# The norms of a two-layer decoder trunk: VectorE's work in a written order, one inverse deviation for both token chunks

## The chip, the cores and the metric

One core of a Trainium2 chip runs the whole kernel. The metric is device time in microseconds of one execution; for the kernel before it is the median of 3 runs. A profile is one further execution, recorded by the hardware profiler; its span runs from the first instruction to the last, and its own time also holds what lies around the span.

TensorE (PE, with PEld for its weight loads) does the matmuls and transposes, VectorE (DVE) elementwise work and reductions, ScalarE (ACT) copies, casts and functions, GpSimd (POOL) the rest, and SyncE (SP) issues nearly all transfers in one queue.

## The reference, cut to what matters

256 tokens of width 1024 go through two layers. Layer 0 is dilated attention, layer 1 attention over a compressed, a selected and a sliding-window branch of one shared set of keys and values. Each layer is followed by 16 experts, of which a token uses 2.

```
def layer_norm(x, g, b):
    mu = mean(x, axis=-1)
    var = mean(square(x - mu), axis=-1)
    return (x - mu) * rsqrt(var + 1e-5) * g + b

for layer in range(2):
    if layer == 0:
        mix = dilated_attention(h, ...)
    else:
        shared_kv = nsa_shared_kv(h, w_kv, ...)      # projections of h: the first work of layer 1
        mix = nsa_attention(h, w_q, ..., *shared_kv)
    h = layer_norm(ALPHA * h + mix, ln_mix_g[layer], ln_mix_b[layer])
    h = layer_norm(ALPHA * h + hier_moe(h, ...), ln_ffn_g[layer], ln_ffn_b[layer])
```

## The kernel before

The tokens are two chunks (c = 0, 1) of 128 partitions. A matmul in the precision that is wanted takes three: each operand is split into a high part (a cast to fp32r, on ScalarE) and a low part (a subtraction, on VectorE), and the products high-high, high-low and low-high are summed. `split` does it for a weight of 128x2048 in four pieces (wh on ScalarE, L251, wl on VectorE, L252), and its results lie in a pool of 4 tiles ("hl"). `projT` and `projN` multiply such a weight with the token matrix: 32 matmuls with wh first, then 16 with wl.

Weights come through one list (`stream`). `take()` gives the next tile of it and loads ahead: as many tiles as `st["ahead"]` says, all from SP's queue in the list's order. Most of them and other wide tiles share a pool of 13 buffers ("u": x, the wkv, w1 and wq weights, lngb, F, KH, KL, VV, qS and others). A load waits in SP's queue until its buffer is free.

A scheduler orders each engine's instructions ahead of time. Inside `tc.manual_schedule(engines=...)` the named engines keep the order of the program text instead; the kernel uses that for TensorE (`PES`) in several places. PSUM tiles for products come from `B("A", ...)`, which here goes round four banks (tags A, A, Y, R).

Between the layers the following happens, in the order of the program. The last experts' outputs are added into x by `scatter(3)` (PSUM tiles sps, L735), which gives the row sums too; 38 matmuls that compute nothing (`awake(38)`) follow on TensorE. For each chunk: the negated mean (`neg_mean`, L477), the squares with their sums (`squares`, ScalarE, L487), z = (x + nm) * g (L956), the inverse deviation by `rstd` (a start value by integer arithmetic and three Newton rounds, on 128x1 columns; on GpSimd for chunk 0 and on VectorE for chunk 1, L495 to L501), z = z * y + b (L960), and 8 transposes of z into two PSUM tiles (hps, L557). Each of these tiles is read three times by `evac`: hTH (ScalarE, L965), hTL (VectorE, L966) and hT (ScalarE, L967). Behind chunk 1's transposes stand 9 more empty matmuls. Then z moves into x as the residual of layer 1 (8 transfers, L978), the first wkv weight is split, and the projections of layer 1 begin (psT, psN).

The norm at the very end (L1230 on) is of the same make without the transposes: the second half of chunk 0's z and chunk 0's inverse deviation are on GpSimd, all else is on VectorE and ScalarE, and four transfers store the output from two queues (L1247).

Of the kernel before, what the change touches and what calls it, by code (L numbers as in the profile page):

```python
# [6 lines left out]
F32 = mybir.dt.float32  # L7
F32R = mybir.dt.float32r
BF16 = mybir.dt.bfloat16
I32 = mybir.dt.int32  # L10
# [6 lines left out]
FIRST = [{("gu", 0, 0): 1}, {}]  # L17
ORDER = [(), tuple(GU0[:6] + DN0 + GU0[6:])]
PES = {mybir.EngineType.PE}
AF = mybir.ActivationFunctionType  # L20
ALU = mybir.AluOpType
AX = mybir.AxisListType
# [2 lines left out]
P = 128  # L25
# [107 lines left out]
def layers(tc, A, out, pools, keep, general):  # L133
# [352 lines left out]
                continue  # L486
            S.activation(junk, r[:, s], AF.Square, bias=nm, scale=1.0, accum_out=q[:, n : n + 1])  # L487

    def rstd(q, y, eng=V):


        vh = sm.tile([P, 1], F32, tag="vh", name="vh")
        yi = sm.tile([P, 1], I32, tag="yi", name="yi")
        t = sm.tile([P, 1], F32, tag="yt", name="yt")
        eng.tensor_tensor(vh, q[:, 0, 0:1], q[:, 0, 1:2], op=ALU.add)  # L495
        eng.tensor_scalar(vh, vh, -0.5 / D, -0.5 * EPS, op0=ALU.mult, op1=ALU.add)
        eng.tensor_scalar(yi, vh.bitcast(I32), -0.5, 519526879.0, op0=ALU.mult, op1=ALU.add)
        y0 = yi.bitcast(F32)
        for _ in range(3):
            eng.tensor_scalar(t, y0, vh, y0, op0=ALU.mult, op1=ALU.mult)  # L500
            eng.tensor_scalar(y, t, 1.5, y0, op0=ALU.add, op1=ALU.mult)  # L501
            y0 = y

    def awake(n, l=None):

        ps = B("S", [P, 512], "idle")
        for _ in range(n):
            if l is None:
                mm(ps, ones, small[:, 0:512], True, True)
            else:  # L510
                mm(ps[:, 0:P], l, l, True, True)
# [112 lines left out]
    def moe_round(layer, hH, hL, r, sums, pos, cc, hook, late, later, rest):  # L624
# [116 lines left out]
        for qd in range(5):  # L741
            if qd < 4:
                oh, C = gather(qd)
            with tc.manual_schedule(engines=PES):
                if qd:
                    ga, gb_, ohT, cslots = whole[qd - 1]
                    ha = hidden(ga, cslots[0], full)
                    if qd > 1:
                        scatter(qd - 2, *whole.pop(qd - 2))
                    if qd == 1:  # L750
                        xg = rows(1, oh)
                    hb = hidden(gb_, cslots[1], full)
                    if qd in (2, 3):
                        xg = rows(qd, oh)
                    if qd < 4:
                        ohT_, cslots_ = places(C)
                else:
                    xg = rows(0, oh)
                    later()
            if qd == 4 and rest:  # L760
                rest()
            with tc.manual_schedule(engines=PES):
                if qd:
                    yH = W(1, [P, 2, D], "yH", F32R)
                    yL = W(2, [P, 2, D], "yL", F32R)
                    down(2 * qd - 2, ha, yH, yL)
                    down(2 * qd - 1, hb, yH, yL)
                    whole[qd - 1] = (ohT, yH, yL)
                if qd < 4:
                    ga = up(2 * qd, xg)  # L770
                    if qd == 0:
                        ohT_, cslots_ = places(C)
                    gb_ = up(2 * qd + 1, xg)
                    whole[qd] = (ga, gb_, ohT_, cslots_)
                else:
                    scatter(3, *whole.pop(3))
                    if layer == 0:
                        awake(38)

    def moe_rest(layer, hH, hL, r, pos, cc):  # L780

# [164 lines left out]
    aL = W(2, [P, 8, T], "hTL", F32R)  # L946
    vT, vH, vL = [t.rearrange("p q (k a) -> p q a k", a=4) for t in (hT, aH, aL)]
    gb, zs = pre["gb"], []
    nms = [neg_mean(sums, c) for c in range(2)]
    for c in range(2):  # L950
        nm = nms[c]
        q = sm.tile([P, 2], F32, tag="sq", name="sq")
        squares(x[:, c], nm, q)
        z = pp.tile([P, D], F32, tag="p", name="z")
        for s in halves:
            V.scalar_tensor_tensor(z[:, s], x[:, c, s], nm, gb[:, 0, s], op0=ALU.add, op1=ALU.mult)  # L956
        y = sm.tile([P, 1], F32, tag="y2", name="y2")
        rstd(q.unsqueeze(1), y, V if c else nc.gpsimd)
        for s in halves:
            V.scalar_tensor_tensor(z[:, s], z[:, s], y, gb[:, 1, s], op0=ALU.mult, op1=ALU.add)  # L960

        def evac(g, ps):
            src = ps.rearrange("p k (a n) -> p k a n", a=2)
            dT, dH, dL = [t[:, 4 * g : 4 * g + 4, 2 * c : 2 * c + 2] for t in (vT, vH, vL)]
            S.copy(dH, src)  # L965
            V.tensor_tensor(dL, src, dH.bitcast(F32), op=ALU.subtract)  # L966
            S.copy(dT, src)  # L967

        with tc.manual_schedule(engines=PES):
            transposeT(z, evac, "A")  # L970
            if c:
                awake(9)
        zs.append(z)

    for a in range(4):
        for half in range(2):
            r0 = 64 * (a % 2) + 32 * half
            nc.sync.dma_start(x[a:P:4, half], zs[a // 2][r0 : r0 + 32])  # L978
    pre["w"] = split(pre["w"])


    st["ahead"] = AH3
# [20 lines left out]
    F = U([P, 2, 2, 512], "F")  # L1003
    nc.gpsimd.memset(F[:, :, 1].rearrange("p b (g n) -> p b g n", g=4)[:, :, :, 120:128], 0.0)
    for br in range(2):
        ps = projT(pre["w"] if br == 0 else split(take()), aH, aL)
        kx = ptp.tile([P, 2, T], F32, tag="pT", name="kx")
        S.copy(kx, ps)
        for g in range(4):
            for par in range(2):  # L1010
                src = kx[64 * (g % 2) : 64 * (g % 2) + 64, g // 2].rearrange("p (n j q) -> p q n j", j=8, q=2)[:, par]
                rows = slice(64 * par, 64 * par + 64)
                for ver in range(2):
                    (nc.gpsimd if g % 2 == par and ver == 1 else V).tensor_tensor(
                        F[rows, br, ver, 128 * g : 128 * g + 128 - 8 * ver].rearrange("p (n j) -> p n j", j=8),
                        src[:, ver:],
                        posT[rows, br, 8 * ver : 8 * ver + 8].unsqueeze(1).to_broadcast([64, 16 - ver, 8]),
                        op=ALU.add,
                    )
# [210 lines left out]

    m.run(hook1)
    h2, gb = U([P, 2, D], "h2"), fin["gb"]
    for c in range(2):
        nm = neg_mean(sums, c)
        q = sm.tile([P, 2], F32, tag="sq", name="sq")
        squares(h[:, c], nm, q)
        for s in halves:
            if (c, s.start) != (0, 512):
                V.scalar_tensor_tensor(h2[:, c, s], h[:, c, s], nm, gb[:, 0, s], op0=ALU.add, op1=ALU.mult)
            else:  # L1240
                nc.gpsimd.tensor_scalar(h2[:, c, s], h[:, c, s], nm, 1.0, op0=ALU.add, op1=ALU.mult)
                nc.gpsimd.tensor_tensor(h2[:, c, s], h2[:, c, s], gb[:, 0, s], op=ALU.mult)
        y = sm.tile([P, 1], F32, tag="y", name="y")
        rstd(q.unsqueeze(1), y, V if c else nc.gpsimd)
        for s, eng in zip(halves, (nc.sync, S)):
            V.scalar_tensor_tensor(h2[:, c, s], h2[:, c, s], y, gb[:, 1, s], op0=ALU.mult, op1=ALU.add)
            eng.dma_start(out[c][:, s], h2[:, c, s])  # L1247


# [67 lines left out]
```

## Time and profile before

| | us |
|---|---|
| median of 3 runs (lowest to highest) | 754.74 (753.69 to 756.08) |
| the profiled execution's own time | 750.46 |
| its span | 748.7 |
| TensorE busy | 715.0 (95%) |
| VectorE busy | 411.1 (55%) |
| ScalarE busy | 319.3 (43%) |
| GpSimd busy | 68.4 (9%) |

Busy time is a sum over the whole span. A TensorE that runs empty matmuls counts as busy. Which wait ends last in a stage is to be read from that stage.

### The profile page before, as it was taken

To read this page: it belongs to the slowest core of one execution; us is meant where nothing else is said; L and a number is where in the kernel's file an instruction comes from. 1 tells how busy PE (TensorE), PEld (TensorE's weight loads), DVE (VectorE), ACT (ScalarE), POOL (GpSimd) and SP (SyncE) were. 2 spreads that over 40 slices of the span, in tenths; PEclk is the share of its full clock that TensorE was granted. 3 is DMA by queue.
4 is the path that set the end of the run, shared out by engine and by line. 5 is a ranking of instruction groups with operands and counts; after the bars stand their busy time and mean duration, and the time that the engine had idled before them with its cause. 6 is when DMAs were issued, how large, how long until landed. Compare 5 with 4: busy or idle time off the path is not lost.

```text
span 748.7 us, 12880 instructions
## 1 busy us (share of the span) xinstructions
PE 715.0 (95%) x5091; PEld 528.4 (71%) x5091; DVE 411.1 (55%) x1055; ACT 319.3 (43%) x710; POOL 68.4 (9%) x117
## 2 busy tenths in 40 slices
PE   8999999999999999999999969999999999999991
PEld 6999999999999988544453439989766554354441
DVE  4665557376555746762332475955875675342335
ACT  5555555455545543331221345545864422230311
POOL 0000000000000000210100023000332211000102
PEclk9999999999999999999999989999999999999996
DMA  7965343433543352789999960014870058799911
GB/s 275 396 278 202 129 167 116 169 113 118 183 158 134 143 225 100 290 321 420 416 417 418 420 232 28 1 57 169 327 292 2 13 213 362 304 365 421 412 47 61
DMA packets 27222, 166.86 MB, mean 223 GB/s; under 512 B 3720, under 2 KB 4232, under 8 KB 9104
## 3 DMA queue, kind: packets, MB, share of 16 engines
q1 hardware_dynamic: 26720, 165.35, 56.3%
q8 instruction: 42, 0.69, 0.4%
q10 hardware_dynamic: 432, 0.59, 0.3%
q14 instruction: 28, 0.23, 0.1%
HBM read 163.83 MB, written 1.05 MB: 220 GB/s over the span
## 4 chain that ended last, share of the span: by engine, by line
PE 87%; DVE 6%; ACT 2%; POOL 1%; issue 1%; DMA 1%; SPq 0%; POOLq 0%; DVEq 0%; ACTq 0%
PE G L167 15%; PE Y L167 7%; PE mix L167 6%; PE po L167 5%; PE gps L167 4%; PE sps L167 3%; PE sc L167 3%; PE ptb L1181 2%; PE s L167 2%; PE pt L420 2%; ACT wh L251 1%; PE psN__665 L167 1%; PE psN__2959 L167 1%; PE psN__2186 L167 1%; PE psN__1419 L167 1%
## 5 line engine op out<-in xcount | busy, mean ns | idle before, releaser
L252 DVE TENSOR_TENSOR wl<-w,wh 128x512 fp32r<-128x512 f32 (+1 forms) x131 | 123.2, 974 | 86.1 <-ACT wh L251 78.5
L251 ACT CAST wh<-w 128x512 fp32r<-128x512 f32 (+1 forms) x131 | 104.0, 843 | 81.3 <-issue 16.2
L167 PE MATMUL G<-w,xg 128*64 128x512 f32 x416 | 92.2, 593 | 0.0
L167 PEld LDWEIGHTS G<-w,xg 128*64 128x64 f32 x416 | 29.7, 137 | 58.1 <-issue 55.5
L167 PE MATMUL Y<-wd,hidT 128*64 128x512 f32 x256 | 57.8, 595 | 0.0
L616 DVE SCALAR_TENSOR_TENSOR sil<-sil,G 128x256 f32<-128x256 f32 x16 | 6.7, 419 | 72.6 <-ACT sil L615 72.6
L167 PEld LDWEIGHTS Y<-wd,hidT 128*64 128x64 f32 x256 | 17.8, 137 | 33.7 <-issue 33.3
L176 DVE TENSOR_TENSOR yL<-Y,yH 128x512 fp32r<-128x512 f32 x32 | 22.1, 692 | 32.5 <-ACT yH L175 32.5
L175 ACT CAST yH<-Y 128x512 fp32r<-128x512 f32 x32 | 18.7, 585 | 36.5 <-PE Y L167 36.5
L621 ACT COPY hidT<-ht 128x256 f32<-128x256 f32 x16 | 6.0, 373 | 64.0 <-PE ht L620 64.0
L1163 ACT ACTIVATE p<-p,nmb 128x128 f32<-128x128 f32 (+1 forms) x64 | 28.5, 448 | 8.2 <-DVE nmb L1162 7.9
L167 PE MATMUL mix<-w,obT 128*128 128x512 f32 x64 | 31.0, 599 | 0.0
L735 DVE SCALAR_TENSOR_TENSOR x<-x,sps 128x512 f32<-128x512 f32 x32 | 21.8, 684 | 15.0 <-PE sps L167 14.6
L615 ACT ACTIVATE sil<-G 128x256 f32<-128x256 f32 x16 | 6.2, 386 | 51.8 <-PE G L167 51.8
L1172 POOL TENSOR_SCALAR p<-p,lb,gates 128x256 f32<-128x256 f32 (+1 forms) x40 | 22.2, 563 | 62.0 <-ACT p L1163 21.2
L167 PE MATMUL gps<-oh,hH 128*128 128x256 f32 x128 | 26.5, 290 | 0.1
L167 PE MATMUL gps<-oh,hL 128*128 128x256 f32 x128 | 26.0, 285 | 0.2 <-DVE hL L869 0.2
L167 PE MATMUL sps<-yH,ohT 128*128 128x512 f32 x64 | 25.9, 405 | 0.0
L405 ACT ACTIVATE p<-p,nm 128x384 f32<-128x384 f32 x32 | 19.6, 614 | 14.2 <-DVE nm L404 14.2
L167 PE MATMUL sps<-yL,ohT 128*128 128x512 f32 x64 | 25.3, 396 | 0.0
L167 PE MATMUL G<-wp,xg 128*64 128x512 f32 x96 | 23.7, 594 | 0.0
L653 ACT ACTIVATE xg<-gps,lnT 128x256 f32<-128x256 f32 x32 | 16.1, 560 | 14.5 <-PE gps L167 13.8
(567 smaller groups left out, 1780.5 us busy)
## 6 DMA issues: line engine op xcount, KB each, us to landing
w<-in_gu SPq DMA_DIRECT2D x52, 1024.0 KB, 11.3
w<-in_a_win SPq DMA_DIRECT2D x35, 1024.0 KB, 4.9
wd<-in_dn SPq DMA_DIRECT2D x32, 1024.0 KB, 8.7
wp<-in_gu SPq DMA_DIRECT2D x24, 512.0 KB, 14.0
w<-in_wkv SPq DMA_DIRECT2D x6, 1024.0 KB, 16.9
w<-in_a_wout SPq DMA_DIRECT2D x4, 1024.0 KB, 4.8
w<-in_w SPq DMA_DIRECT2D x4, 1024.0 KB, 19.9
w<-in_wq SPq DMA_DIRECT2D x4, 1024.0 KB, 4.7
```

Source lines behind the costliest of these rows:

```text
L167: nc.tensor.matmul(out, l, r, start=start, stop=stop)
L175: S.copy(dstH, src)
L176: V.tensor_tensor(dstL, src, dstH.bitcast(F32), op=ALU.subtract)
L251: S.copy(h[:, s], w[:, s])
L252: low.tensor_tensor(l[:, s], w[:, s], h[:, s].bitcast(F32), op=ALU.subtract)
L405: S.activation(w, w, AF.Exp, bias=nm, scale=-1.0, accum_out=l)
L420: nc.tensor.transpose(pt[:, b], ptiles[pr][:, hh, b * P : (b + 1) * P], ident)
L653: S.activation(xg[:, k], banks4[k // 2][:, k % 2], AF.Identity, bias=b_, scale=g_)
L735: V.scalar_tensor_tensor(r[:, c, s], r[:, c, s], 1.0 if qd else ALPHA, ps, op0=ALU.mult, op1=ALU.add, accum_out=sums[:, c, n : n + 1])
L1163: S.activation(dst, dst, AF.Exp, bias=nm[:, hl, b : b + 1], scale=-1.0, accum_out=l[:, hl, b : b + 1])
L1172: eng.tensor_scalar(dst, dst, l[:, hl, b : b + 1], gates[:, c, 1 + b, 4 * g + hl : 4 * g + hl + 1], op0=ALU.mult, op1=ALU.mult)
L1181: nc.tensor.transpose(pt[:, b], ptiles[pr][:, hh, b * P : (b + 1) * P], ident)
```

## The change

The norm between the layers puts VectorE's instructions in the order of the text (`DVES`). Both chunks' squares and z come first, then one `rstd` on 128x2 columns for both, then the four scalings, then the evacuations of all transposes. The copies hT stand behind the other evacuations of both chunks, and the splits of the first two wkv weights, with the `take()` of the second, behind these. `rstd` runs on VectorE alone; with two columns a Newton round takes two products of tensors and one scalar_tensor_tensor, where one column takes two tensor_scalars. The empty matmuls ahead of the transposes are 31 instead of 38. The norm at the end uses one `rstd` for both chunks too, but its order is left to the scheduler; GpSimd keeps its half of z there.

```
--- before.py
+++ after.py
@@ -17,6 +17,7 @@
 FIRST = [{("gu", 0, 0): 1}, {}]
 ORDER = [(), tuple(GU0[:6] + DN0 + GU0[6:])]
 PES = {mybir.EngineType.PE}
+DVES = {mybir.EngineType.DVE}
 AF = mybir.ActivationFunctionType
 ALU = mybir.AluOpType
 AX = mybir.AxisListType
@@ -486,19 +487,25 @@
                 continue
             S.activation(junk, r[:, s], AF.Square, bias=nm, scale=1.0, accum_out=q[:, n : n + 1])
 
-    def rstd(q, y, eng=V):
-
-
-        vh = sm.tile([P, 1], F32, tag="vh", name="vh")
-        yi = sm.tile([P, 1], I32, tag="yi", name="yi")
-        t = sm.tile([P, 1], F32, tag="yt", name="yt")
-        eng.tensor_tensor(vh, q[:, 0, 0:1], q[:, 0, 1:2], op=ALU.add)
-        eng.tensor_scalar(vh, vh, -0.5 / D, -0.5 * EPS, op0=ALU.mult, op1=ALU.add)
-        eng.tensor_scalar(yi, vh.bitcast(I32), -0.5, 519526879.0, op0=ALU.mult, op1=ALU.add)
+    def rstd(q, y):
+
+
+        n = y.shape[1]
+        vh = sm.tile([P, n], F32, tag="vh", name="vh")
+        yi = sm.tile([P, n], I32, tag="yi", name="yi")
+        t = sm.tile([P, n], F32, tag="yt", name="yt")
+        V.tensor_tensor(vh, q[:, :, 0], q[:, :, 1], op=ALU.add)
+        V.tensor_scalar(vh, vh, -0.5 / D, -0.5 * EPS, op0=ALU.mult, op1=ALU.add)
+        V.tensor_scalar(yi, vh.bitcast(I32), -0.5, 519526879.0, op0=ALU.mult, op1=ALU.add)
         y0 = yi.bitcast(F32)
         for _ in range(3):
-            eng.tensor_scalar(t, y0, vh, y0, op0=ALU.mult, op1=ALU.mult)
-            eng.tensor_scalar(y, t, 1.5, y0, op0=ALU.add, op1=ALU.mult)
+            if n == 1:
+                V.tensor_scalar(t, y0, vh, y0, op0=ALU.mult, op1=ALU.mult)
+                V.tensor_scalar(y, t, 1.5, y0, op0=ALU.add, op1=ALU.mult)
+            else:
+                V.tensor_tensor(t, y0, vh, op=ALU.mult)
+                V.tensor_tensor(t, t, y0, op=ALU.mult)
+                V.scalar_tensor_tensor(y, t, 1.5, y0, op0=ALU.add, op1=ALU.mult)
             y0 = y
 
     def awake(n, l=None):
@@ -775,7 +782,7 @@
                 else:
                     scatter(3, *whole.pop(3))
                     if layer == 0:
-                        awake(38)
+                        awake(31)
 
     def moe_rest(layer, hH, hL, r, pos, cc):
 
@@ -946,37 +953,44 @@
     aL = W(2, [P, 8, T], "hTL", F32R)
     vT, vH, vL = [t.rearrange("p q (k a) -> p q a k", a=4) for t in (hT, aH, aL)]
     gb, zs = pre["gb"], []
-    nms = [neg_mean(sums, c) for c in range(2)]
-    for c in range(2):
-        nm = nms[c]
-        q = sm.tile([P, 2], F32, tag="sq", name="sq")
-        squares(x[:, c], nm, q)
-        z = pp.tile([P, D], F32, tag="p", name="z")
-        for s in halves:
-            V.scalar_tensor_tensor(z[:, s], x[:, c, s], nm, gb[:, 0, s], op0=ALU.add, op1=ALU.mult)
-        y = sm.tile([P, 1], F32, tag="y2", name="y2")
-        rstd(q.unsqueeze(1), y, V if c else nc.gpsimd)
-        for s in halves:
-            V.scalar_tensor_tensor(z[:, s], z[:, s], y, gb[:, 1, s], op0=ALU.mult, op1=ALU.add)
-
-        def evac(g, ps):
-            src = ps.rearrange("p k (a n) -> p k a n", a=2)
-            dT, dH, dL = [t[:, 4 * g : 4 * g + 4, 2 * c : 2 * c + 2] for t in (vT, vH, vL)]
-            S.copy(dH, src)
-            V.tensor_tensor(dL, src, dH.bitcast(F32), op=ALU.subtract)
+    q = sm.tile([P, 2, 2], F32, tag="sq", name="sq")
+    y = sm.tile([P, 2], F32, tag="y2", name="y2")
+
+    with tc.manual_schedule(engines=DVES):
+        nms = [neg_mean(sums, c) for c in range(2)]
+        for c in range(2):
+            squares(x[:, c], nms[c], q[:, c])
+            z = pp.tile([P, D], F32, tag="p", name="z")
+            for s in halves:
+                V.scalar_tensor_tensor(z[:, s], x[:, c, s], nms[c], gb[:, 0, s], op0=ALU.add, op1=ALU.mult)
+            zs.append(z)
+        rstd(q, y)
+        for c in range(2):
+            for s in halves:
+                V.scalar_tensor_tensor(zs[c][:, s], zs[c][:, s], y[:, c : c + 1], gb[:, 1, s], op0=ALU.mult, op1=ALU.add)
+        whole = []
+        for c in range(2):
+
+            def evac(g, ps):
+                src = ps.rearrange("p k (a n) -> p k a n", a=2)
+                dT, dH, dL = [t[:, 4 * g : 4 * g + 4, 2 * c : 2 * c + 2] for t in (vT, vH, vL)]
+                S.copy(dH, src)
+                V.tensor_tensor(dL, src, dH.bitcast(F32), op=ALU.subtract)
+                whole.append((dT, src))
+
+            with tc.manual_schedule(engines=PES):
+                transposeT(zs[c], evac, "A")
+                if c:
+                    awake(9)
+        for dT, src in whole:
             S.copy(dT, src)
-
-        with tc.manual_schedule(engines=PES):
-            transposeT(z, evac, "A")
-            if c:
-                awake(9)
-        zs.append(z)
+        w0, w1_ = pre["w"], take()
+        pre["w"] = [split(w0), split(w1_)]
 
     for a in range(4):
         for half in range(2):
             r0 = 64 * (a % 2) + 32 * half
             nc.sync.dma_start(x[a:P:4, half], zs[a // 2][r0 : r0 + 32])
-    pre["w"] = split(pre["w"])
 
 
     st["ahead"] = AH3
@@ -1003,7 +1017,7 @@
     F = U([P, 2, 2, 512], "F")
     nc.gpsimd.memset(F[:, :, 1].rearrange("p b (g n) -> p b g n", g=4)[:, :, :, 120:128], 0.0)
     for br in range(2):
-        ps = projT(pre["w"] if br == 0 else split(take()), aH, aL)
+        ps = projT(pre["w"][br], aH, aL)
         kx = ptp.tile([P, 2, T], F32, tag="pT", name="kx")
         S.copy(kx, ps)
         for g in range(4):
@@ -1230,20 +1244,21 @@
 
     m.run(hook1)
     h2, gb = U([P, 2, D], "h2"), fin["gb"]
+    q = sm.tile([P, 2, 2], F32, tag="sq", name="sq")
+    y = sm.tile([P, 2], F32, tag="y", name="y")
     for c in range(2):
         nm = neg_mean(sums, c)
-        q = sm.tile([P, 2], F32, tag="sq", name="sq")
-        squares(h[:, c], nm, q)
+        squares(h[:, c], nm, q[:, c])
         for s in halves:
             if (c, s.start) != (0, 512):
                 V.scalar_tensor_tensor(h2[:, c, s], h[:, c, s], nm, gb[:, 0, s], op0=ALU.add, op1=ALU.mult)
             else:
                 nc.gpsimd.tensor_scalar(h2[:, c, s], h[:, c, s], nm, 1.0, op0=ALU.add, op1=ALU.mult)
                 nc.gpsimd.tensor_tensor(h2[:, c, s], h2[:, c, s], gb[:, 0, s], op=ALU.mult)
-        y = sm.tile([P, 1], F32, tag="y", name="y")
-        rstd(q.unsqueeze(1), y, V if c else nc.gpsimd)
+    rstd(q, y)
+    for c in range(2):
         for s, eng in zip(halves, (nc.sync, S)):
-            V.scalar_tensor_tensor(h2[:, c, s], h2[:, c, s], y, gb[:, 1, s], op0=ALU.mult, op1=ALU.add)
+            V.scalar_tensor_tensor(h2[:, c, s], h2[:, c, s], y[:, c : c + 1], gb[:, 1, s], op0=ALU.mult, op1=ALU.add)
             eng.dma_start(out[c][:, s], h2[:, c, s])
```

## Rows read from the trace of the kernel before

**Rows 1.** The page, busy time, its share and instructions of each engine.
```profile
PE 715.0 (95%) x5091; PEld 528.4 (71%) x5091; DVE 411.1 (55%) x1055; ACT 319.3 (43%) x710; POOL 68.4 (9%) x117
```

**Rows 2.** Windows by stage: length, busy us and count by engine, granted clock, DMA.
```profile
439.30:446.20 6.90, 0.00 (x0) 0.00 (x0) 6.79 (x16) 3.40 (x4) 0.00 (x0) 0.71 0.73 242
...
520.00:540.00 20.00, 19.20 (x148) 15.19 (x148) 17.37 (x100) 17.00 (x72) 4.78 (x10) 1.00 0.78 306
...
640.00:700.00 60.00, 60.00 (x314) 29.33 (x312) 21.39 (x48) 13.85 (x33) 2.42 (x4) 1.00 0.92 371
...
730.00:748.70 18.70, 2.87 (x13) 2.04 (x11) 10.31 (x27) 3.04 (x8) 5.06 (x11) 0.66 0.16 61
```

**Rows 3.** Timeline of TensorE between the layers: start, us, line, instruction, count, idle before.
```profile
429.67 8.38 PE L167 MATMUL idle<-small,ones 128*128 128x512 bf16 x38
437.93 1.32 PE L557 MATMUL hps<-cs,z 128*128 128x128 f32 x8
446.25 1.97 PE L557 MATMUL hps<-cs,z 128*128 128x128 f32 x8 [7.01 <-DVE z L960]
...
450.31 0.47 PE L167 MATMUL psT__4603<-hTH,wh 128*128 128x256 f32 x1
```

**Rows 4.** The chain that ended last, behind the norm: start, us, what.
```profile
450.66 5.74 PE psT__4603 L167 x48
...
492.32 5.96 PE psT__5060 L167 x48
```

**Rows 5.** Timeline of VectorE, between the layers and later.
```profile
437.12 1.41 DVE L960 SCALAR_TENSOR_TENSOR z<-z,y,lngb 128x512 f32<-128x512 f32 x2 [2.99 <-POOL y L501]
...
442.14 0.68 DVE L252 TENSOR_TENSOR wl<-w,wh 128x512 fp32r<-128x512 f32 x1
442.74 2.00 DVE L966 TENSOR_TENSOR hTL<-hps,hTH 128x512 fp32r<-128x512 f32 x2
...
445.20 0.21 DVE L501 TENSOR_SCALAR y<-yt,y 128x1 f32<-128x1 f32 x1
...
478.90 0.69 DVE L322 TENSOR_TENSOR KL<-psT__4760,KH 64x512 fp32r<-64x512 f32 x1
```

**Rows 6.** Timeline of ScalarE between the layers.
```profile
433.47 0.19 ACT L487 ACTIVATION_READ_ACCUMULATOR junk<-x,nmean 128x1 f32 x1
...
438.67 2.00 ACT L965 CAST hTH<-hps 128x512 fp32r<-128x512 f32 x2 [4.51 <-PE hps L557]
443.82 2.02 ACT L967 COPY hT<-hps 128x512 f32<-128x512 f32 x2 [3.14 <-DVE hTL L966]
```

**Rows 7.** Groups of small VectorE instructions in the first router: busy us, mean ns.
```profile
L500 DVE TENSOR_SCALAR yt<-yi,vh 128x1 f32<-128x1 f32 x2 | 0.5, 272 | 0.0
...
L495 DVE TENSOR_TENSOR vh<-sq 128x1 f32<-128x1 f32 x2 | 0.3, 160 | 1.6 <-ACT junk L487 1.6
...
L600 DVE SCALAR_TENSOR_TENSOR wt<-wt 128x1 f32<-128x1 f32 x2 | 0.3, 152 | 0.0
```

**Rows 8.** Timelines of ScalarE and VectorE in the last norm.
```profile
735.75 0.18 ACT L487 ACTIVATION_READ_ACCUMULATOR junk<-x,nmean 128x1 f32 x1
...
738.28 1.41 DVE L1246 SCALAR_TENSOR_TENSOR h<-h,y,lngb 128x512 f32<-128x512 f32 x2 [3.08 <-POOL y L501]
...
740.28 0.15 DVE L495 TENSOR_TENSOR vh<-sq 128x1 f32<-128x1 f32 x1
...
742.52 1.42 DVE L1246 SCALAR_TENSOR_TENSOR h<-h,y,lngb 128x512 f32<-128x512 f32 x2
```

**Rows 9.** Timelines of SP's queue, of GpSimd, and VectorE's next read of x.
```profile
443.23 6.17 SPq L978 DMA_DIRECT2D x<-z  x8
...
489.67 0.33 SPq L229 DMA_DIRECT2D w<-in_wq  x1
...
446.92 0.15 POOL L1004 MEMSET F<- 128x64 f32 x1 [9.84 <-DVE z L960]
...
581.91 0.69 DVE L463 SCALAR_TENSOR_TENSOR x<-x,mix 128x512 f32<-128x512 f32 x1 [3.33 <-PE mix L167]
```

## The prediction

> **What bounds the kernel now.** I read the page first, for which engine is the limit. TensorE is busy for 715.0 of 748.7 us [rows 1], so time can be won only where TensorE idles or runs matmuls that compute nothing. The windows by stage then say where that is [rows 2]: 60.00 of 60 us are matmuls in the second layer's experts, but from 439.30 to 446.20 us, between the layers, TensorE does nothing, and the last 18.7 us hold only 2.87 us of matmuls. These two places are the two norms that the change touches.
>
> TensorE's own list of the first [rows 3] shows the pattern. When layer 0 has ended, 38 fillers (`awake(38)`) start at 429.67; the 8 transposes of token chunk 0 stand at 437.93, those of chunk 1 only at 446.25, and the first projection of layer 1 (psT) starts at 450.31. So for 20.6 us no layer works. The releaser in the row of chunk 1 is VectorE's z.
>
> Then VectorE and ScalarE in the same stretch. VectorE waits 2.99 us, to 437.12, for GpSimd's inverse deviation of chunk 0 [rows 5]. After that the scheduler has put six weight subtractions (wl, the last of them at 442.14) and two hTL evacuations between the small steps of chunk 1's inverse deviation: its last step stands at 445.20, although ScalarE's squares had all ended at 433.47 + 0.19 = 433.66 [rows 5, 6]. Nearly 12 us lie between the squares and a value that takes about 2 us to work out.
>
> **The norm between the layers, step by step.** Up to the squares nothing changes: 433.66.
>
> *One inverse deviation.* It now runs on VectorE for both chunks: 3 head steps and 3 rounds of (product, product, add-and-multiply), 12 instructions of 128x2. No row shows them at that size. The nearest are 128x1: 0.160 us for a product of two tensors, 0.152 for a scalar_tensor_tensor [rows 7]. The gap from one step to the next comes from the last norm: 9 steps from 740.28 to 742.52 [rows 8] are 2.24 us, of which 3 x 0.15 + 3 x 0.27 + 3 x 0.21 = 1.89 are the steps [rows 5, 7, 8], so 0.04 each. Then 12 x (0.155 + 0.04) = 2.3 us. Bounds: 1.9 without gaps, 3.7 if each costs what the dearest small form costs (0.272 + 0.04). I take 2.3, since the forms are those of the rows and a second column is hardly work. Both chunks then have it at 433.7 + 2.3 = 436.0, where before chunk 0 had it at 437.1 and chunk 1 at 445.4.
>
> Here a rule speaks against the change. By the rows the old form, 9 steps with two column operands in most, takes 2.24, and the new one with 12 steps about the same, since two plain products (0.16 each) replace a 0.272. The Trainium skill (VectorE: DVE Perf Modes, Rules for kernel authors) says to keep the number of instructions in such a chain small, as each pays its pipeline drain. By that the price would be 2.24 x 12/9 = 3.0, and the gain 0.7 less in each norm.
>
> *Scaling and transposes.* Four scalings of z follow with nothing between them, 0.75 for the first and 0.66 for each further one (two in 1.41, [rows 5]): done at 436.8, 437.5, 438.1, 438.8. `awake(31)` ends at 429.67 + 31 x 0.22 = 436.5 (38 of them lead to 437.93, [rows 3]), just ahead of the first transposes. So the 7 fillers less (1.5 us) win nothing by themselves; they make room for what VectorE has ready earlier. All transposes are done by 439.4, the 9 fillers behind them by 441.4.
>
> *Evacuation.* ScalarE's hTH stands 0.75 us behind a group's first transpose (437.93 to 438.67, [rows 3, 6]) and takes 1.0: four from 437.6 to 441.6. VectorE's hTL, 1.0 each [rows 5], go from the last scaling on: 439.8, 440.8, 441.8, 442.8. The hT copies now stand behind all else: the first from 441.6 to 442.6. It counts, because the rotation of four "A" banks gives the first projection the bank of the first transpose group, which is free after its hT. So psT starts at 442.6; hTL for its first matmuls is there at 441.8, that for the ninth (0.12 each, [rows 4]) at 442.8. Before it was 450.3: **7.7 us less**. Bounds: 8.9 if the fillers (441.4) end last, 4.7 if psT has to wait for all four hT copies (445.6).
>
> *The weight subtractions.* All eight now stand behind hTL, 0.60 apart [rows 5]: the first weight's are done at 442.8 + 2.4 = 445.2. They are first used 32 of 48 matmuls into psT, 5.74 x 32/48 = 3.8 us after its start [rows 4], at 446.4. The second weight's are done at 447.6 and used near 452. Cover 1.2 and 4 us; without it psT would wait one for one. Cost taken: nothing.
>
> *The second weight's earlier take().* It reaches one tile further down the list of loads while 12 ahead are allowed: the fourth wq load, issued at 489.67 before, now stands in SP's queue ahead of the 8 moves of z into x, which went out from 443.23 [rows 9]. It waits for the third buffer to come free, the second weight's at 447.6, and the moves go out some 4.5 us later. x is next read at 581.91 [rows 9], so over 100 us of attention cover it.
>
> *Granted clock.* In the 6.9 us of idle TensorE the clock averaged 0.71 [rows 2]. With the two levels 1.00 and 0.50 that is full clock for 0.42 of it, some 2.9 us, and half after. The new gaps are 0.4 us before the first transposes and 1.2 before psT, both shorter, so everything above is priced at full clock.
>
> **The last norm.** Before, VectorE waits 3.08 us for GpSimd, to 738.28, scales chunk 0, does the last half of z, works out chunk 1's inverse deviation and scales it, to 742.52 + 1.42 = 743.94 [rows 8]. Now the last half of z fits into that idle time, the squares end at 735.93 [rows 8], the 12 steps at 738.3, and four scalings (0.75 + 3 x 0.66) at 741.1: 2.8 us less. The four stores now leave within 2 us instead of in two pairs 4 us apart. I take 0.2 for queueing, at most one scaling's 0.7. **2.6 us less**; bounds 0.7 (the steps at 3.7, the queue at 0.7) and 3.2 (steps at 1.9, no queue).
>
> **Sum.** 7.7 + 2.6 = 10.3. Behind psT nothing is tied to absolute time: the projections follow one another, loads wait for buffers that compute frees [rows 9], and the experts are full of matmuls [rows 2]. So the shift goes through to the end. The profiled execution took 750.46 with a span of 748.7; it would give 740.2 and 738.4. The median of the runs shown is 754.74, 4.28 above; the same 10.3 off gives **744.4**.
>
> **The rivals.**
>
> *A, as summed:* 744.4, by the likelier bounds 742 to 746.
>
> *B, evacuation holds the projection back.* ScalarE is not ordered by hand. If it takes hT copies between the hTH ones, or psT gets the bank that is copied last, the norm wins 4.7: 754.74 - 4.7 - 2.6 = 747.4. For it: hT waited for hTL before, 3.14 us [rows 6]. Against: the copies come last in the program, and the rotation gives the first bank.
>
> *C, given back behind the norm.* The engines' order in layer 1's attention is made anew. If new stalls there eat what the norm won, only the end's 2.6 stays: 752.1, at the edge of no change. For it: TensorE idles for 0.8 us in 520 to 540 already [rows 2], so waits end last there at times. Against: these would have to grow tenfold, with the same dependences, all earlier by the same amount.
>
> *D, slower, for want of buffers.* There are 13 wide buffers. F took the one that gb left (its memset waits for z, [rows 9]). With the fourth wq weight loaded early, x, four wkv, four w1 and four wq weights hold all 13: F must wait for the third wkv weight's split, KL for the fifth's instead of the fourth's. That costs once KL keeps the key projection's PSUM bank until the first query projection wants it, at 492.32 before [rows 4]; KL was done at 479.6 [rows 5]. So there are 12.7 us of room; beyond it each us costs one, and after 10.3 more the kernel is slower than now. One split more is 4 x 0.60 = 2.4 us of VectorE: far from that point. If it comes, 757 or more.
>
> **How the numbers follow.** A 0.70, B 0.14, C 0.12, D 0.04. About 0.3% (2.3 us) is what a measurement of this kernel can tell from no change. A, B and half of C are faster by more: 0.90. The other half of C is the same: 0.06. D is slower: 0.04. The range goes from 741.0 (8.9 and 3.2, and a stall or two less behind) to 749.0 (B, with the steps at 3.0 in both norms), which leaves out C and D, 0.16.
>
> **What the profile afterwards should show.** No small steps on GpSimd; 12 on VectorE at some 0.16, ended by 436.0; the transposes of both chunks between 436.8 and 439.5; a granted clock of 1.00 from there into the projections; psT at 442.6, just behind the first hT copy; projections without gaps; three wq loads ahead of the moves of x; VectorE's last scaling ending near 733.4 (741.1 - 7.7) and a span of 738.4. The prediction is wrong if psT starts after 445.6, if TensorE shows new gaps between psT and the experts, or if the small steps cost over 0.3 each.

## The result: 744.24 us, and the profile after

The changed kernel takes 744.24 us (median of 4 executions, 740.47 to 746.41); the kernel before takes 754.90 us beside it (4 executions, 753.69 to 756.08). The ratio is 0.9854, with a 95% interval of 0.9807 to 0.99. The forecast was 744.4, the range 741.0 to 749.0. The terms of the sum before the first projection hold nearly one by one; behind it one did not, and that the median was met so closely is partly luck, as the runs below show.

The profiled execution took 746.41 us, with a span of 744.6. Busy times first, to set beside [rows 1]:

```profile
PE 717.5 (96%) x5084; PEld 530.8 (71%) x5084; DVE 411.5 (55%) x1061; ACT 319.0 (43%) x710; POOL 61.4 (8%) x99
```

GpSimd has 18 instructions less (two inverse deviations of 9 steps), and VectorE 6 more (two of 12 where there were two of 9). Sums say no more than that. TensorE's timeline between the layers answers to [rows 3]:

```profile
432.65 6.86 PE L168 MATMUL idle<-small,ones 128*128 128x512 bf16 x31
439.68 2.64 PE L564 MATMUL hps<-cs,z 128*128 128x128 f32 x16 [0.16 <-DVE z L970]
442.16 2.10 PE L168 MATMUL idle<-small,ones 128*128 128x512 bf16 x9
445.29 0.39 PE L168 MATMUL psT__4600<-hTH,wh 128*128 128x256 f32 x1 [1.03 <-ACT hT L986]
...
479.26 1.45 PE L168 MATMUL psN__4941<-wl,hTH 128*128 128x256 f32 x10 [0.37 <-DVE wl L253]
```

All 16 transposes now stand together, behind the fillers, and waited 0.16 us for z; 7.01 us were waited for chunk 1's before. The first projection waits 1.03 us for an hT copy, and there is a new gap of 0.37 us at the last row; both come back below.

In this execution everything in the norm is 2.98 us later: the first fillers stand at 432.65, not at 429.67 [rows 3]. The delay arises in the first 30 us; the chain of this execution has a late weight there (start, us, what),

```profile
12.70 13.54 DMA w<-in_a_win
```

where the chain of before has

```profile
2.14 6.79 DMA w<-in_a_win
```

A second profile of the changed kernel doesn't have that delay: its first fillers stand at 429.87. So the stages are measured from their own start:

| us | before | after | after, a second profile |
|---|---|---|---|
| first filler to first projection (psT) | 20.64 | 12.64 | 12.62 |
| last scatter matmul of layer 0 to the compression's matmuls (hd) | 55.76 | 48.28 | 48.26 |
| last scatter matmul of all to the last scaling's end | 11.46 | 8.65 | 8.66 |
| last scaling's end to the end of the span | 4.76 | 4.93 | 5.23 |

The compression (hd) is the first work behind layer 1's six projections of keys and values; it reads F, which VectorE and GpSimd make of the first two. So the norm between the layers won 8.00 us at the first projection, of which 7.5 are left at hd; the last norm won 2.81, of which 0.2 to 0.5 went to the stores. VectorE's timeline shows the chain inside the norm, beside [rows 5]:

```profile
436.46 0.15 DVE L497 TENSOR_TENSOR vh<-sq 128x2 f32<-128x2 f32 x1
...
438.61 0.16 DVE L508 SCALAR_TENSOR_TENSOR y<-yt,y 128x2 f32<-128x2 f32 x1
438.87 2.74 DVE L970 SCALAR_TENSOR_TENSOR z<-z,y,lngb 128x512 f32<-128x512 f32 x4
441.57 4.02 DVE L978 TENSOR_TENSOR hTL<-hps,hTH 128x512 fp32r<-128x512 f32 x4
445.49 2.50 DVE L253 TENSOR_TENSOR wl<-w,wh 128x512 fp32r<-128x512 f32 x4
448.53 2.50 DVE L253 TENSOR_TENSOR wl<-w,wh 128x512 fp32r<-128x512 f32 x4 [0.54 <-ACT wh L252]
```

The 12 steps run from 436.46 to 438.61 + 0.16 = 438.77, without a wait for another engine; the scalings, the evacuations and the first weight's subtractions follow with none either. ScalarE, beside [rows 6]:

```profile
435.17 0.19 ACT L488 ACTIVATION_READ_ACCUMULATOR junk<-x,nmean 128x1 f32 x1
...
440.43 3.90 ACT L977 CAST hTH<-hps 128x512 fp32r<-128x512 f32 x4 [5.07 <-PE hps L564]
444.09 3.98 ACT L986 COPY hT<-hps 128x512 f32<-128x512 f32 x4
447.81 4.28 ACT L252 CAST wh<-w 128x512 fp32r<-128x512 f32 x8
```

The squares end at 435.36, 1.1 us ahead of the 12 steps: VectorE's z, not the squares, is what they follow. The hT copies hold ScalarE until 448, and the wh casts of the second weight come so late behind them that VectorE waits 0.54 us in its last row above. The last norm on VectorE, beside [rows 8]:

```profile
734.50 0.16 DVE L497 TENSOR_TENSOR vh<-sq 128x2 f32<-128x2 f32 x1
...
736.67 0.16 DVE L508 SCALAR_TENSOR_TENSOR y<-yt,y 128x2 f32<-128x2 f32 x1
736.93 2.74 DVE L1261 SCALAR_TENSOR_TENSOR h<-h,y,lngb 128x512 f32<-128x512 f32 x4
```

The wait of 3.08 us for GpSimd is gone; again 12 steps (2.33 us) and four scalings in a row.

### The profile page after: what moved, and what is told of

It is laid out like the page before. It is cut to its first block, busy times and chain, and to the rows that moved or that the text cites. A ratio compares the mean times of both kernels' runs of the same rounds, so it can differ in the third digit from the quotient of the medians.

```text
span 744.6 us, 12852 instructions
## 1 busy us (share of the span) xinstructions
PE 717.5 (96%) x5084; PEld 530.8 (71%) x5084; DVE 411.5 (55%) x1061; ACT 319.0 (43%) x710; POOL 61.4 (8%) x99
## 4 chain that ended last, share of the span: by engine, by line
PE 83%; DVE 8%; ACT 3%; DMA 3%; issue 1%; SPq 0%; POOL 0%; DVEq 0%; ACTq 0%; POOLq 0%
PE G L168 15%; PE Y L168 8%; PE mix L168 6%; PE po L168 5%; PE gps L168 4%; PE sps L168 4%; DMA w<-in_a_win 3%; PE sc L168 3%; PE ptb L1195 2%; PE s L168 2%; PE pt L421 2%; ACT wh L252 1%; PE psT__5265 L168 1%; PE psN__2186 L168 1%; PE psN__1419 L168 1%
```

## The experiments

Times are medians, ratios are to the kernel before on the same chip: 753.80 us (17 executions) beside the first four kernels below, 753.83 (9) beside the free order, the 38 empty matmuls, the other bank and the gate products dealt out, 753.74 (10) beside the other four. Where a stage is compared, it is one profiled execution, from the last scatter matmul (hd) or from the first filler (psT), and "later" and "earlier" are against the changed kernel.

### The changed kernel again

> The changed kernel once more. In its first profile the stretch from the first empty matmul to the first projection of layer 1 took 12.64 us (before: 20.64) and that from the last scatter matmul to the last scaling 8.65 us (before: 11.46); but layer 0 ended 2.98 us later than before, and the granted clock fell to half from about 507 to 513 us with TensorE busy, which cost 3.0 us. Theory: both of these belong to one execution and not to the change. Then 12.6 and 8.65 come again, and a profile without the late start and the fall has a span near 738.6; median 10 to 11 us below before. Rival: the earlier arrival of layer 1 causes the fall; then it stands again behind the first query projections, at the same distance from the first projection, and the span stays at 741 or more.

741.66 us (6 executions, 740.48 to 747.52), ratio 0.9852 [0.9821, 0.9884]. The stage table is the same to 0.02 us up to the last scaling, so the norm is not what spreads the executions over 7 us. A fall of the clock in layer 1 is 3 us of it (the section on the hardware), and this profile has the fall too (span 742.0); the late weight of the first profile can be another 3. The rest is open.

### Each norm alone

The old norm at the end, the new one between the layers:

```
-    rstd(q, y)
-    for c in range(2):
+        y = sm.tile([P, 1], F32, tag="y", name="y")
+        rstd1(q.unsqueeze(1), y, V if c else nc.gpsimd)
...
```

`rstd1` is the old `rstd` of one column.

> The changed kernel with the last norm as before (chunk 0's inverse deviation on GpSimd). Theory: the two norms add up. First empty matmul to first projection 12.6 us, last scatter matmul to last scaling back at 11.4 to 11.5, so 2.6 to 2.8 us slower than the changed kernel and some 8 us faster than before. Rival: the last norm hides behind the stores (their queue and landing), so that its undoing costs under 0.7 us.

746.01 us, ratio 0.9901 [0.9878, 0.9924]. All four executions have a mean clock of 0.987 to 0.988, as those with the fall have, so they are set beside the kernel before, of which nearly all have it too. First filler to psT is 12.62 as in the changed kernel, and from the last scatter to the last scaling it is 11.47 as before. The wait is back, on VectorE's timeline of this kernel:

```profile
733.80 1.42 DVE L1275 SCALAR_TENSOR_TENSOR h<-h,y,lngb 128x512 f32<-128x512 f32 x2 [3.10 <-POOL y L523]
```

The other way round, the kernel before with the new last norm alone (the last hunk of the diff, and an `rstd` of two columns for it):

> The kernel before with only the last norm changed. Theory: first empty matmul to first projection 20.6 us, last scatter matmul to last scaling 8.65 us, 2.6 us faster than before (0.35%). Rival, stores hide it: within 0.7 us of before.

751.12 us (12 executions), ratio 0.9964 [0.9945, 0.9983]. Against before the parts are 753.80 - 746.01 = 7.8 and 753.80 - 751.12 = 2.7 us: the sum of 10.5 is the whole within the spreads (10.04 below), and the norms don't disturb one another.

One forecast missed: first filler to psT took 21.19 us here, 0.55 more than in the profile of before, although this norm is the old one. The 9 empty matmuls behind chunk 1's transposes took 3.18 us instead of 2.64. In the changed kernel they take 2.10, and the granted clock shows why; before, from the end of the idle to psT, it is 0.65:

```profile
446.20:450.30 4.10, 4.04 (x17) 2.65 (x18) 2.45 (x3) 2.66 (x3) 0.15 (x1) 0.65 0.95 321
```

Here it is 0.57 from 446.2 to 450.9, and in the changed kernel 1.00. So the old norm pays for its idle TensorE twice: in waiting, and in half clock behind it.

### The written order without sharing, and sharing without the order

Two of them on VectorE, one for each chunk, in the written order:

```
-        rstd(q, y)
+        for c in range(2):
+            rstd(q[:, c : c + 1], y[:, c : c + 1])
```

> The changed kernel, but in the norm between the layers two inverse deviations of one column each, one after the other on VectorE, still in the written order and ahead of all scalings. Theory: the written order, not the sharing, carries the gain. 18 steps of 0.249 us (2.24 for 9 in the trace of before) instead of 12 in 2.36 us make 4.5 us, so the first projection comes 2.1 us later: 14.7 us after the first empty matmul, 2.1 us slower than the changed kernel, 8 us faster than before. Rival: the sharing carries it, because the chain of small steps costs far more than its rows say when it is doubled: 4 us or more lost.

744.85 us, ratio 0.9879 [0.9855, 0.9903]. First filler to psT takes 14.43 us, 1.81 more; at hd 1.2 are left. TensorE's transposes wait for it:

```profile
438.15 2.65 PE L564 MATMUL hps<-cs,z 128*128 128x128 f32 x16 [1.98 <-DVE z L971]
```

One inverse deviation for both, but VectorE left to the scheduler:

```
-    with tc.manual_schedule(engines=DVES):
+    if True:
```

> The changed kernel, but with VectorE's order in the norm between the layers left to the scheduler, which puts seven weight subtractions (wl, 0.61 us each) between the halves of z and the steps of the shared inverse deviation. Theory: the written order carries part of the gain by keeping these behind hTL. The steps start when z ends in either case, so the first projection comes 7 x 0.61 = 4.3 us later: 16.9 us after the first empty matmul instead of 12.6 (before: 20.6). Rival: one inverse deviation for both chunks on VectorE is all that counts and the subtractions fill idle time: 12.6 to 13.2 us.

744.53 us, ratio 0.9882 [0.9867, 0.9897]. VectorE's timeline shows what the order keeps out, and TensorE's what it costs:

```profile
434.59 0.16 DVE L497 TENSOR_TENSOR vh<-sq 128x2 f32<-128x2 f32 x1
434.66 0.69 DVE L253 TENSOR_TENSOR wl<-w,wh 128x512 fp32r<-128x512 f32 x1
...
439.38 2.74 DVE L970 SCALAR_TENSOR_TENSOR z<-z,y,lngb 128x512 f32<-128x512 f32 x4
```

```profile
440.19 3.29 PE L564 MATMUL hps<-cs,z 128*128 128x128 f32 x16 [3.72 <-DVE z L970]
```

Two weight subtractions stand ahead of the first of the 12 steps and five among them; the scalings start 4.8 us after that step, where in the changed kernel it is 438.87 - 436.46 = 2.4. psT comes 3.56 us later than in the changed kernel (16.18 us after the first filler; forecast 16.9), and hd 3.9 later. So taking back the written order loses almost half of the 8.0, taking back the sharing under a quarter. Taking back the cut of the empty matmuls loses 1.09, and taking back the moved copies next to nothing (both below). These losses need not add up. What is left to the 8.0, some 1.5, no run parts: chunk 0's deviation off GpSimd is in it, and the half clock that is gone.

### The empty matmuls

`awake(38)` in place of `awake(31)`:

> The changed kernel with 38 empty matmuls ahead of the transposes instead of 31. Theory: they end 7 x 0.22 = 1.5 us later, at 8.4 us, where the transposes would have stood at 7.0: the first projection comes 1.4 us later, at 14.0 us after the first empty matmul. So cutting them wins nothing by itself but 1.4 of the 8.0 us would be lost without it. Rival: VectorE's hTL, which starts after the last scaling, sets the first projection whatever the transposes do: no change, 12.6 us.

743.71 us, ratio 0.9855 [0.9831, 0.988]; psT 1.09 us later (forecast 1.4), hd 0.5. None at all (`awake(31)` taken out):

> The changed kernel without the 31 empty matmuls ahead of the transposes (the 9 behind them stay). Theory: TensorE idles 7 us there, the granted clock falls after some 3 us, and transposes, fillers and the start of the first projection run at half clock; the first projection starts within 1 us of before, hd comes 1 to 2.5 us later: 49 to 50.5 us after the last scatter matmul instead of 48.0. Rival: TensorE has room there, since VectorE and the copies set the first projection: no change.

741.91 us, ratio 0.9846 [0.9824, 0.9869]; hd 0.4 us later. My forecast of 1 to 2.5 missed. The windows of this kernel show why it costs so little:

```profile
434.00:436.00 2.00, 0.00 (x0) 0.00 (x0) 1.67 (x8) 0.00 (x0) 0.00 (x0) 0.50 0.13 53
440.00:442.00 2.00, 1.97 (x9) 0.77 (x7) 0.93 (x2) 2.00 (x3) 0.00 (x0) 1.00 0.96 397
```

The clock does fall while TensorE idles (0.50 in the column before the last two), and is 1.00 again from 440 on. The timeline of TensorE shows what half clock cost in between:

```profile
436.27 3.54 PE L564 MATMUL hps<-cs,z 128*128 128x128 f32 x16 [6.87 <-DVE z L968]
439.86 1.89 PE L168 MATMUL idle<-small,ones 128*128 128x512 bf16 x8
441.78 0.39 PE L168 MATMUL psT__4568<-hTH,wh 128*128 128x256 f32 x1
442.90 0.39 PE L168 MATMUL psT__4568<-hTL,wh 128*128 128x256 f32 x1 [0.74 <-DVE hTL L976]
```

The transposes take 0.9 us more than the 2.64 of the changed kernel, and the second matmul of psT waits for the hTL that are later by it.

### Evacuation and the first projection's bank

The first projection gets another first bank, the spare one (S), so that it need not wait for the first hT copy:

```
+        banks(A="SAAYR", S="S", T="T", O="O")
         w0, w1_ = pre["w"], take()
```

> The changed kernel with another PSUM bank for the first projection (one that the empty matmuls leave), so that it need not wait for the first hT copy. Theory: that copy sets its start; without it the hTL of its first matmuls does (1.0 us after the fourth-last, about 0.6 us earlier): 12.0 us after the first empty matmul instead of 12.6, and the fillers end just before. Rival: hTL or the fillers set it, the bank only seems to: 12.6 us as before.

742.94 us, ratio 0.9841 [0.9822, 0.9861]. The first matmul of psT stands 1.36 us earlier, but the second waits for hTL, so that the second projection starts 0.67 us earlier and hd 0.3. TensorE's timeline:

```profile
441.51 0.39 PE L168 MATMUL psT__4600<-hTL,wh 128*128 128x256 f32 x1 [0.33 <-DVE hTL L978]
```

hTL is next in line, so no more than this 0.7 us is to be won at the bank. The hT copies back in their old place, each right behind its hTL:

```
-                whole.append((dT, src))
+                S.copy(dT, src)
...
-        for dT, src in whole:
-            S.copy(dT, src)
```

> The changed kernel with the copy hT beside the other two evacuations of its group, as in the kernel before; the scheduler then puts the first hT ahead of the last hTH on ScalarE. Theory: the first projection's bank is free 0.9 us earlier and the last hTH, and with it the hTL of its ninth matmul, comes 0.9 to 1.0 us later; the two cancel, the first projection ends within 0.4 us and hd within 0.3 us. So the moved copies carry none of the gain. Rival: they do, and 1 us or more is lost.

742.81 us, ratio 0.9842 [0.9815, 0.9869]; hd 0.3 us later. On ScalarE one copy goes ahead of the last hTH:

```profile
436.92 2.97 ACT L977 CAST hTH<-hps 128x512 fp32r<-128x512 f32 x3 [5.08 <-PE hps L564]
439.65 1.16 ACT L979 COPY hT<-hps 128x512 f32<-128x512 f32 x1
440.57 1.17 ACT L977 CAST hTH<-hps 128x512 fp32r<-128x512 f32 x1
```

So the bank is free sooner (the first matmul of psT stands 0.91 us earlier, counted from the last scatter matmul) and the last hTL is later (the second projection starts 0.06 later), as forecast; moving the copies is worth 0.3 us at most.

### The gate products dealt out

The profiles of the changed kernel and of most variants above show TensorE at half clock behind the gate products (gx, the section on the hardware). Here each of these 18 matmuls follows one of the next query projection's instead of standing in a row:

```
     def products(ps, three, other=()):
...
                        mm(ps[:, j], l, r, low == j == k == n == 0, bool(low) and j == 1 and k == 7)
+                        if other:
+                            mm(*other.pop(0))
```

> The changed kernel with the 18 gate products (gx, 48 columns each, recorded as 36) dealt out between the matmuls of the third query projection instead of in a row ahead of it. In the profiles with a fall of the granted clock in layer 1 it came during gx, with the old and with the new norm. Theory: gx in a row brings the fall, in some executions and not in others, and this is what spreads the runs by 3 us. Dealt out, the clock stays at 1.00 through this stage, no run lies near 743.8 or 746, and the median is near 740.5. Rival: the wait of 0.8 us ahead of it (for hrep) or the transfers that start there bring it: then the fall stays in most executions, with the median near 742 and a spread of 3 us.

740.87 us (5 executions, 740.19 to 742.31), ratio 0.9833 [0.982, 0.9847]. The same edit on the kernel before:

> The kernel before with the gate products dealt out between the matmuls of the third query projection, nothing else. Theory: most executions of the kernel before hold the fall of the clock during gx, worth 3.3 us, and its first profile did not (750.46 against medians of 753.8 to 754.9; the other executions near it ran at a mean clock of 0.987 instead of 0.983). Then all executions lie near 750.2, 3.4 us under the kernel before, and the changed kernel with the same edit (740.87) is 9.4 us under this one: the change's gain without the fall. Rival: the fall is the change's own cure, and the kernel before stays at 753 to 754.

750.91 us (5 executions, 750.34 to 751.90), ratio 0.9962 [0.9948, 0.9975]. Between these two kernels, neither of which shows the fall there, the change is worth 750.91 - 740.87 = 10.04 us (on two chips, on which the kernel before takes 753.74 and 753.83). Last, the changed kernel with both this and the other bank:

> The changed kernel with the gate products dealt out and the first projection in another PSUM bank. Theory: the two add up only in part, since behind the first projections VectorE's queue (weight subtractions, F, KL) ends last: the first projection 0.6 us earlier, the compression's matmuls (hd) 0.3 us earlier, median 740.2 to 740.8, no fall of the clock. Rival: the 0.6 goes through: 740.0 or less.

740.55 us (5 executions, 739.58 to 741.01), ratio 0.9822 [0.9808, 0.9835]; hd comes 0.46 us earlier than in the changed kernel. It is the fastest of all, but its lead over 740.87 is within their spreads.

## Why the prediction was right, and where it was not

*The 12 steps.* Forecast 2.3 us from the rows; measured 438.77 - 436.46 = 2.31, at 0.16 each and a step every 0.195. The Trainium skill's rule (VectorE: DVE Perf Modes, Rules for kernel authors: keep the number of chained instructions small), read as an equal price for each instruction, would have made it 3.0 here. The trace doesn't bear that price out: what an instruction does counted as much as how many there are, since products of two tensors (0.16) replaced the form with two column operands (0.272, [rows 7]).

*When they start.* I let them start at the end of the squares, 3.99 us behind the first filler. The squares end 435.36 - 432.65 = 2.71 behind it now, since the written order puts the first chunk's mean earlier (with the order left free they end 3.99 behind again), but VectorE's own four z keep it until 436.46, 3.81 behind. The result is 0.2 from the forecast, for another reason than the one given: that is luck.

*`awake(31)`* was to win nothing by itself and make room. With 38 again psT is 1.09 us later and hd 0.5: that is what the room is worth.

*Transposes and evacuation.* All as forecast within half a microsecond: transposes right behind the fillers, hTH in one row of four, the first hT copy last before psT. Forecast 442.6 in the time of [rows 3], measured 445.29 - 2.98 = 442.31: the norm won 8.0, not 7.7. That the bank sets it is shown by the other bank (the projection starts 1.36 earlier and then waits for hTL). Rival B needed psT to wait for a later copy; it didn't.

*Weight subtractions: "cost taken: nothing".* This held. The first weight's are done at 445.49 + 2.50 - 2.98 = 445.0 (forecast 445.2) and the second's at 448.1 (447.6), and neither the first nor the second projection waits for them.

*"So the shift goes through to the end"* is the term that was put at nothing and was not: 0.5 us came back between psT and hd, and the new gap of 0.37 in TensorE there is one of the prediction's own signs of being wrong. The gap's releaser is a subtraction of the sixth weight, in VectorE's queue behind the second projection:

```profile
457.15 2.50 DVE L253 TENSOR_TENSOR wl<-w,wh 128x512 fp32r<-128x512 f32 x4 [3.26 <-ACT wh L252]
462.91 3.30 DVE L253 TENSOR_TENSOR wl<-w,wh 128x512 fp32r<-128x512 f32 x4 [3.27 <-ACT wh L252]
466.13 7.81 DVE L1028 TENSOR_TENSOR F<-kx,bm 64x128 f32<-64x128 f32 x24
...
478.53 0.68 DVE L253 TENSOR_TENSOR wl<-w,wh 128x512 fp32r<-128x512 f32 x1
```

These are the fourth and the fifth weight's subtractions, then F's 24 additions. The last input of F is there at 457.84, but F starts 8.3 us behind it, because the scheduler's new order puts it behind the fifth weight; that weight's subtractions start 0.10 us behind the end of the third projection (457.05 + 5.76 = 462.81), and VectorE idles meanwhile. Before, F stands behind the fourth weight's, 2.2 us after its last input (462.99):

```profile
462.25 3.01 DVE L252 TENSOR_TENSOR wl<-w,wh 128x512 fp32r<-128x512 f32 x4 [2.75 <-ACT wh L251]
465.19 7.81 DVE L1014 TENSOR_TENSOR F<-kx,bm 64x128 f32<-64x128 f32 x24
```

Counted from psT, F starts at 20.84 us instead of 14.88, and what follows it on VectorE is late for the sixth projection. The 0.54 us that VectorE waited for the second weight's wh has no part in it: behind it VectorE idles 3.26 us twice, and the kernel with the hT copies in their old place, which has no such wait, has a gap of 0.60 at the same matmuls. The kernels in which psT starts 1.1 to 1.8 us later have no gap there and win part of that back by hd (1.09 to 0.5, 1.81 to 1.2), which fits a queue on VectorE that ends at its own time. This is read from the traces; no run moves F ahead of the fifth weight. It is rival C's mechanism, an order made anew, at a fifteenth of its size.

*The loads.* Of SP's queue and GpSimd, beside [rows 9]:

```profile
441.68 9.70 SPq L230 DMA_DIRECT2D w<-in_wq  x3
451.43 3.86 SPq L993 DMA_DIRECT2D x<-z  x6
...
453.94 0.15 POOL L1018 MEMSET F<- 128x64 f32 x1 [28.12 <-DVE wl L253]
```

Three wq loads stand ahead of the moves of x, as forecast, and the moves go out 451.43 - 2.98 - 443.23 = 5.2 us later (forecast 4.5), at no cost. F's memset waits for a weight's subtraction, which is the beginning of rival D. It did not decide: it ends 12 us ahead of VectorE's first addition to F.

*The clock in the norm* was 1.00 from 442.20 to 445.20, as forecast; the run without fillers, with 0.50 there, lost 0.4 by hd.

*The last norm.* Forecast 2.8 less the stores' 0.2; measured 2.81 less 0.17 and, in the second profile, 0.47.

*The sum* was 10.3. Measured: 7.5 and 2.3 to 2.6, which is 9.8 to 10.1; the two kernels with the gate products dealt out say 10.04. The 0.3 that the norm won beyond the forecast and the 0.5 that came back behind it nearly cancel, which is luck too.

*The step that failed: "the median of the runs shown is 754.74, 4.28 above; the same 10.3 off gives 744.4".* The 4.28 us was carried over unexplained, as if every execution had it. It is mostly half clock at the gate products, which nearly every execution of the kernel before has and its profiled one had not. The forecast from the profiled execution, 740.2 with a span of 738.4, is near what the five executions of the changed kernel without that loss took: 740.47, 740.48, 740.59, 741.21 and 742.11, with spans of 738.6 to 740.3. The other five, by their mean clock, have it, and the median of each group of runs depends on how many there are: 744.24 in the first, 741.66 in the second. That 744.4 agrees with the first is chance to this extent.

## What to carry to other kernels

Where a short chain of small instructions stands between two stages, look for what the scheduler puts between them: without the written order 3.6 us were lost at the first projection, more than with two chains instead of one (1.8). Price small instructions by rows of their own form, not by count. Behind the stage look at what the scheduler's order has become for work that you did not touch. And when the profiled execution is not the median one, find out where the difference lies before a sum made on the one is carried to the other.

## What the runs showed of the hardware that I had not expected

TensorE's clock fell to half with TensorE fully busy. The kernel before, in its profiled execution, has full clock there; windows (the column after the five engines is the granted clock):

```profile
508.00:512.00 4.00, 4.00 (x34) 3.81 (x33) 3.45 (x10) 3.08 (x10) 0.00 (x0) 1.00 0.03 6
```

The changed kernel, profiled at 746.41 us:

```profile
503.00:507.00 4.00, 4.00 (x33) 3.89 (x32) 3.43 (x9) 3.76 (x12) 0.00 (x0) 0.91 0.02 4
507.00:513.00 6.00, 6.00 (x27) 5.82 (x28) 2.60 (x8) 0.25 (x1) 0.00 (x0) 0.50 0.47 176
```

That is 1.2 in place of 2.4 GHz for six microseconds in which TensorE idled 0.00. What it did just before is the gate products: 18 matmuls of 48 columns, one behind the other, in two records each. In the chains, before has

```profile
507.77 4.33 PE gx L167 x36
512.10 5.95 PE psT__5280 L167 x48
```

and the changed kernel

```profile
503.29 5.36 PE gx L168 x36
508.65 7.92 PE psT__5265 L168 x48
```

so the fall costs 13.28 - 10.28 = 3.0 us. It is not peculiar to the change: the kernel before with only the last norm new, profiled at 751.28 us, has it as well,

```profile
512.00:518.00 6.00, 6.00 (x28) 5.82 (x28) 2.66 (x7) 1.39 (x3) 0.00 (x0) 0.50 0.48 176
```

With the 18 matmuls dealt out among those of 256 columns, the window that holds them all, in the changed kernel with that edit,

```profile
500.20:506.50 6.30, 6.30 (x54) 6.00 (x52) 4.87 (x12) 3.63 (x11) 0.00 (x0) 1.00 0.02 4
```

stays at 1.00. For executions without a profile only the mean clock and the time speak. The kernel before has a mean clock of 0.981 to 0.983 and 752.97 us or more in 33 of 36, and 0.987 with 749.97 to 750.57 in three; its profiled execution took 750.46. The changed kernel has 0.985 to 0.989 in five of ten (742.95 to 747.52 us) and 0.992 to 0.993 in the other five (740.47 to 742.11). With the products dealt out all executions lie at the higher value or near it: 0.991 to 0.993 in five of the changed kernel, 0.985 to 0.987 in five of the one before, 0.993 to 0.995 in five with the other bank too.

So without the row the fall behind it doesn't come. The row alone doesn't decide: eight of the eleven profiled kernels with it show the fall, and before, the free order and the one without fillers don't. Two other things that stand there don't decide either. The wait of some 0.77 us (for hrep in most) that stands 4 to 6 us ahead of the row is in every profile, and the transfers behind the row are in before at full clock too (a DMA share of 0.63 from 512 to 518). Nor is the row the only place: without the fillers, and with the hT copies in their old place, the clock is also at 0.50 from 499 to 500 us, ahead of the row, with TensorE busy throughout. Which execution gets the fall, and why fewer of the changed kernel's do, stays open.
